# Plain projection pairs by single channel tile in two PSUM banks, and three more pairs by seven products, in an encoder layer

## Chip, cores and metric

The kernel runs on one core of one Trainium2 chip. The metric is the device time of one execution in microseconds (us); lower is better. The time before is a median of three runs.

## Reference: what is computed

One layer of an encoder over 1024 + 256 tokens of width 2048, in float32:

```python
h    = rmsnorm(x, norm_w)
P    = h @ w_in          # q, k, v, gate for the neighbourhood attention (4 x 1024 columns),
                         # qk (2048), v, o, z for the mLSTM (3 x 1024), and 16 gate columns
att  = neighbourhood_attention(q, k, v, bias) * silu(gate)        # 8 heads of 128
mem  = rmsnorm(bidirectional_mlstm(silu(conv(qk)), v, gates)) * sigmoid(o) * silu(z)   # 4 heads of 256
y    = rmsnorm(x + concat(att, mem) @ w_out, final_norm_w)
```

## The kernel before

All matrix products take float32 operands split into a high and a low part, and each product is three matmuls (high by high, high by low, low by high). The 1280 tokens are two groups: group A with 768 tokens and group B with 512. The projection's columns for q, k, gate, qk, o and z are 56 channel tiles of 128 columns, handled two at a time as a pair named by its first tile: QT0 = 0 (attention q), KT0 = 8 (k), GT0 = 16 (gate), QK0 = 24 (mLSTM qk), OT0 = 40, ZT0 = 48. The value columns come in eight units of `proj_v`.

The program has these stages, in this order on TensorE:

1. **Group A, seven products.** `first_tiles` (L282) does pairs 0 and 2 plainly. `pair_a` (L464) does all others with Strassen's seven products of half-size blocks instead of eight; pairs 4 and 6 (QT0 + 4 and QT0 + 6) are its first two. For each of four weight pieces GpSimd forms sums of blocks (L508). For the pairs listed in `SECOND` (L38) the sums 5, 6, 7 and 3 are also stored to DRAM (`sD`, L522), one DMA of 128 KB each, sixteen for a pair. The finished pair is post-processed while the next one runs.
2. **Group B, start.** `proj_v(4)` and `proj_v(0)`, the plain pair 0, and the mLSTM's gates (L1437 to L1443).
3. **Group B, seven products.** `pair_s` (L1338) does the nine pairs of `SECOND`. Each of seven steps loads 512 KB, either a block of the weights or a stored sum, and issues 24 matmuls of 256 columns (L1375), 168 for a pair.
4. **Group B, plain, together with the attention and the mLSTM.** `proj_v` (L705) issues 192 matmuls of 256 columns per unit. `proj_pair` (L646) takes both channel tiles of a pair at once: for each of four weight pieces of 512 KB it splits two halves and issues 24 matmuls of 512 columns (L658), alternating between two PSUM banks, 96 for a pair. The attention (`na_sample`, `na_prompt`) and the mLSTM (`ml_units`) are cut into short units, which `run` (L1300) emits with high priority; the plain pairs and values are emitted earlier with low priority. A scheduler orders each engine's instructions when the program is built: plain matmuls fill TensorE between the steps of the units. Four `late_gate` calls (L691), two plain pairs each, come last and can also be drawn forward as filler.
5. **Output projection.** `product` (L1603) with two rounds of seven products, 1680 matmuls of 512 columns (L1609). Its operands are read back from DRAM by `mix_block` (L1486) on GpSimd's DMA queue into the memory that the attention's tiles held before.

PSUM has eight banks in two pools: tag `pr` with three, tag `a` with five (L73). Stages 1 and 3 and the plain pairs use `pr`; the attention and the mLSTM use `a`, as does every second pair of stage 3. An attention block takes banks for its scores (L767), its transposed probabilities (L783) and its outputs (L820 for the sample, L878 for the prompt). A head's query and key tile (`nqk`, L793 and L838) has one buffer: the loads for the prompt part of a head can start only when the sample part's scores are done, and the other way round.

The square in the mLSTM's output norm (L1254) writes an unused result into a tile of the pool `sml`, which has six buffers and also holds the gate operands that are loaded from DRAM.

Of the kernel before, what the change touches and what calls it, by code (L numbers as in the profile page):

```python
# [38 lines left out]
    GT0, QK0 + 8, GT0 + 2, QK0, KT0, GT0 + 4, KT0 + 2, GT0 + 6, KT0 + 4,  # L39
# [6 lines left out]
def kernel(  # L46
# [26 lines left out]
    def bank(tag, name):  # L73
        return ps.tile([P, 512], F32, tag=tag, name=name, bufs=3 if tag == "pr" else 5)
# [207 lines left out]
    def first_tiles():  # L282
        names = ("pr", "pr", "pr", "a", "a", "a", "a", "a")
# [362 lines left out]
    def proj_pair(n1, X, late=False):  # L646
        pb = [bank("pr", f"pc{n1}_{j}") for j in range(2)]
        for r in range(4):
            raw = w_piece(w_in[n1 // 2, r], f"{n1}_{r}")
            t = [w_split(raw, j * 512, j * 512 + 512, f"{n1}_{r}{j}") for j in range(2)]  # L650
            for f_ in range(2):
                for q in range(2):
                    xs = X.get(8 * f_ + 2 * r + q)
                    c = (2 * f_ + q) * P
                    first, last = r + f_ + q == 0, r == 3 and f_ == 1 and q == 1
                    for j, passes in enumerate((FORTH, FORTH[::-1])):
                        for m, (wi, xi) in enumerate(passes):
                            PE.matmul(  # L658
                                pb[j], t[j][:, wi, c : c + P], xs[xi],
                                start=first and m == 0, stop=last and m == 2,  # L660
                            )
        out = []
        for j in range(2):
            o = po(f"pco{n1}_{j}")
            if QK0 <= n1 < OT0:
                ct = n1 - QK0 + j
                DM.dma_start(o[:, 0:4], qb[ct])
                for z in (260, 518):
                    G.memset(o[:, z : z + 2], 0.0)
                out_scaled(  # L670
                    o[:, 4:].rearrange("p (s c) -> p s c", s=2)[:, :, :256],
                    pb[j].rearrange("p (s c) -> p s c", s=2),
                    rbs[1].rearrange("p (s c) -> p s c", s=2), n1,
                )
                for _ in conv_b(o, ct):
                    pass
                continue
            o = o[:, :GB]
            out_scaled(o, pb[j], rbs[1], n1)
# [25 lines left out]
    def proj_v(u, X):  # L705
# [54 lines left out]
    def sml(name, n=256, dt=F32):  # L760
        return ap.tile([P, 260], dt, tag="sml", name=name, bufs=6)[:, :n]
# [29 lines left out]
    def na_sample(h):  # L791
# [28 lines left out]
        b = bank("a", f"{nm}o")  # L820
# [12 lines left out]
    def na_prompt(h):  # L833
# [13 lines left out]
        def block(c4):  # L847
# [30 lines left out]
            b = bank("a", f"{n2}o")  # L878
# [173 lines left out]
    def ml_units(sq, h, gates):  # L1052
# [98 lines left out]
        def out_unit(J):  # L1151
# [84 lines left out]
            for e in range(2):  # L1236
# [17 lines left out]
                jk = sml(f"{n2}jk{e}")  # L1254
# [83 lines left out]
    def pair_s(n1, tag, bg):  # L1338
        nm = f"S{n1}"
        bx, by, bz = (bank(tag, f"{nm}b{i}") for i in "xyz")  # L1340
# [105 lines left out]
    for i, n in enumerate(SECOND):  # L1446
        bg = pair_s(n, ("pr", "a")[i % 2], bg)
# [4 lines left out]
    for i in range(ML_H):  # L1452
        for u in (("v", 4 + i), QK0 + 8 + 2 * i, QK0 + 2 * i, ("v", i), QT0 + 2 * i, KT0 + 2 * i):
# [3 lines left out]
            elif u not in SECOND and u != QT0:  # L1457
                proj_pair(u, X)
    def paced(units, n):
# [182 lines left out]
    slots = iter(("aaaaa" "ppp") * 8)  # L1642

    def p_banks(p, j):
        return [bank("pr" if next(slots) == "p" else "a", f"po{p}_{j}_{i}") for i in range(NT)]
# [130 lines left out]
```

## Time and profile before

| What | Value |
|---|---|
| Median of three runs | 2568.87 us (2566.79 to 2569.39) |
| The profiled execution | 2567.36 us |
| Span from its first to its last instruction | 2565.5 us |
| Mean granted TensorE clock | 0.998 |
| TensorE matmul busy | 2534.0 us (99%) |
| VectorE busy | 1968.9 us (77%) |
| ScalarE busy | 1336.5 us (52%) |
| GpSimd busy | 610.6 us (24%) |
| DMA traffic | 503.03 MB |

In the profile, PE is TensorE's matmuls, PEld its weight loads, DVE is VectorE, ACT is ScalarE, POOL is GpSimd and SPq the queue of the sync engine, which issues most DMAs. PEclk is the clock that TensorE was granted, 1.00 being full. A line such as L658 is the line of the program above. The view of the chain follows the work that ended last back to its start; the view of the waits adds up the idle time of an engine by what ended it; the view of windows gives each engine's busy time in stretches of the span, with the share of the time in which the 16 DMA engines were busy.

### The profile page before, as it was taken

To read this page: it belongs to the slowest core of one execution; us is meant where nothing else is said; L and a number is where in the kernel's file an instruction comes from. 1 tells how busy PE (TensorE), PEld (TensorE's weight loads), DVE (VectorE), ACT (ScalarE), POOL (GpSimd) and SP (SyncE) were. 2 spreads that over 40 slices of the span, in tenths; PEclk is the share of its full clock that TensorE was granted. 3 is DMA by queue.
4 is the path that set the end of the run, shared out by engine and by line. 5 is a ranking of instruction groups with operands and counts; after the bars stand their busy time and mean duration, and the time that the engine had idled before them with its cause. 6 is when DMAs were issued, how large, how long until landed. Compare 5 with 4: busy or idle time off the path is not lost.

```text
span 2565.5 us, 44500 instructions
## 1 busy us (share of the span) xinstructions
PE 2534.0 (99%) x15054; PEld 2367.4 (92%) x15054; DVE 1968.9 (77%) x4029; ACT 1336.5 (52%) x3041; POOL 610.6 (24%) x909
## 2 busy tenths in 40 slices
PE   8999999999999999999999999999999999999998
PEld 8999999999999999999999999899988887788886
DVE  8768878888978798888875875876855665879695
ACT  8534544444444444475655665665745553344444
POOL 0434555444444444510000000100100104000001
PEclk9999999999999999999999999999999999999999
DMA  6545454635433332476778877978867839636227
GB/s 214 170 145 183 155 182 139 185 114 189 138 120 124 105 130 102 134 245 214 230 235 292 284 250 266 304 234 275 286 199 249 280 126 374 204 128 215 85 87 254
DMA packets 303483, 503.03 MB, mean 196 GB/s; under 512 B 48752, under 2 KB 191256, under 8 KB 303256
## 3 DMA queue, kind: packets, MB, share of 16 engines
q1 hardware_dynamic: 299096, 484.46, 57.4%
q0 software_dynamic: 4160, 15.73, 1.6%
q8 instruction: 119, 1.95, 0.3%
q14 instruction: 108, 0.88, 0.1%
HBM read 373.13 MB, written 126.95 MB: 195 GB/s over the span
## 4 chain that ended last, share of the span: by engine, by line
PE 77%; DMA 3%; DVE 2%; ACT 0%; issue 0%; SPq 0%; POOL 0%; ACTq 0%; POOLq 0%; DVEq 0%
PE pc L658 16%; PE po L1609 15%; PE pv L736 5%; PE A52b L274 1%; PE A44b L274 1%; PE A40b L274 1%; PE A48b L274 1%; PE A20b L274 1%; PE A50b L274 1%; PE A42b L274 1%; PE A18b L274 1%; PE A54b L274 1%; PE A70b L274 1%; PE A68b L274 1%; PE A36b L274 1%; PE A46b L274 1%
## 5 line engine op out<-in xcount | busy, mean ns | idle before, releaser
L1609 PE MATMUL po<-wo,mo 128*128 128x512 f32 x1620 | 377.8, 394 | 2.5 <-ACT wo L165 2.2
L1609 PEld LDWEIGHTS po<-wo,mo 128*128 128x128 f32 x1620 | 305.0, 188 | 74.5 <-ACT wo L165 3.0
L166 DVE TENSOR_TENSOR ws<-wr,ws 128x512 fp32r<-128x512 f32 x152 | 105.0, 700 | 50.8 <-ACT ws L165 50.1
L165 ACT CAST ws<-wr 128x512 fp32r<-128x512 f32 x152 | 92.5, 617 | 68.0 <-PE pc L658 56.0
L165 ACT CAST mo<-mb 128x640 fp32r<-128x640 f32 x72 | 52.0, 726 | 97.4 <-PE po L1609 79.1
L116 POOL TENSOR_SCALAR rs<-rs 128x1 f32<-128x1 f32 x10 | 3.4, 342 | 350.4 <-DVE rs L1589 350.3
L166 DVE TENSOR_TENSOR mo<-mb,mo 128x640 fp32r<-128x640 f32 x72 | 58.6, 820 | 30.5 <-ACT mo L165 30.2
L1558 DVE TENSOR_TENSOR y<-y,po 128x512 f32<-128x512 f32 x90 | 58.3, 682 | 11.7 <-PE po L1609 11.5
L165 ACT CAST mo<-ms 128x640 fp32r<-128x640 f32 x40 | 28.9, 726 | 59.7 <-PE po L1609 34.2
L166 DVE TENSOR_TENSOR wsv<-wr_v,wsv 128x512 fp32r<-128x512 f32 x64 | 44.4, 699 | 12.6 <-ACT wsv L165 12.4
L165 ACT CAST wsv<-wr_v 128x512 fp32r<-128x512 f32 x64 | 38.9, 616 | 22.7 <-PE pv L736 11.5
L413 DVE SCALAR_TENSOR_TENSOR pcv<-pco,cw_sb,pcv 128x516 f32<-128x516 f32 x48 | 36.3, 757 | 8.0 <-ACT pcv L407 7.9
L1572 ACT ACTIVATE jk<-y 128x512 f32<-128x512 f32 x40 | 25.2, 631 | 33.0 <-DVE y L1558 32.8
L166 DVE TENSOR_TENSOR mo<-ms,mo 128x640 fp32r<-128x640 f32 x40 | 32.7, 819 | 8.0 <-ACT mo L165 7.8
L129 ACT ACTIVATE xq<-xq 128x1024 f32<-128x1024 f32 x20 | 21.2, 1061 | 29.6 <-DMA xq<-in_xtok_dram 27.1
L1077 POOL MEMSET mls_0v<- 128x2 f32 x4 | 0.4, 102 | 145.0 <-DVE S_dt.float L166 119.9
L274 PE MATMUL fb<-xg,fw 128*128 128x384 f32 x192 | 34.6, 334 | 0.0
L251 DVE TENSOR_TENSOR pco<-pc,rstdb 128x512 f32<-128x512 f32 x30 | 20.6, 686 | 18.0 <-PE pc L658 17.9
L274 PEld LDWEIGHTS fb<-xg,fw 128*128 128x128 f32 x192 | 33.4, 188 | 0.0
L1521 DVE TENSOR_TENSOR ms<-mb,mb 128x640 f32<-128x640 f32 x40 | 32.7, 818 | 0.0
L774 DVE CUSTOM_DVE_ANT_0 nap_0st<-nap_0s,nap_0bt 128x384 f32<-128x384 f32 x32 | 17.7, 554 | 19.2 <-PE nap_0s L769 8.7
L1488 POOL DMA_DIRECT2D mb<-mx x32 | 17.7, 556 | 59.1 <-DVE ws L166 24.7
(2655 smaller groups left out, 8497.4 us busy)
## 6 DMA issues: line engine op xcount, KB each, us to landing
wr<-in_w_in_dram SPq DMA_DIRECT2D x76, 512.0 KB, 4.4
wr_v<-in_w_in_dram SPq DMA_DIRECT2D x32, 512.0 KB, 4.6
wb<-in_w_o_dram SPq DMA_DIRECT2D x48, 256.0 KB, 3.1
xq<-in_xtok_dram SPq DMA_DIRECT2D x20, 512.0 KB, 4.3
mb<-mx POOLq DMA_DIRECT2D x32, 320.0 KB, 8.2
wr_wp<-in_w_o_dram SPq DMA_DIRECT2D x16, 512.0 KB, 3.8
vS<-vo SPq DMA_DIRECT2D x24, 256.0 KB, 4.9
nap_0bt<-in_rpb_tab_dram SPq DMA_DIRECT2D x32, 192.0 KB, 4.1
```

The lines of the kernel that those rows point to most:

```text
L129: S.activation(raw, raw, AF.Square, accum_out=ssq[g][:, t, q : q + 1])
L165: S.copy(hi, src)
L166: V.tensor_tensor(lo, src, f(hi), op=ALU.subtract)
L251: V.tensor_tensor(o, src, rb, op=ALU.mult)
L274: PE.matmul(o, w(a_), x(b_), start=first and m == 0, stop=last and m == 2)
L413: V.scalar_tensor_tensor(dst[:, a:n], src[:, a + j - pad : n + j - pad], cw_sb[:, ct, j : j + 1], dst[:, a:n], op0=ALU.mult, op1=ALU.add,)
L658: PE.matmul(pb[j], t[j][:, wi, c : c + P], xs[xi], start=first and m == 0, stop=last and m == 2,)
L736: PE.matmul(outs[tt], xs[:, tt * P : (tt + 1) * P], t[:, wi, q * w : (q + 1) * w], start=first and m == 0 and (gates or tt % 2 == 0), stop ...
L1521: V.tensor_tensor(t, x, y_, op=op)
L1558: V.tensor_tensor(Y[p, q, tt], Y[p, q, tt], bk, op=op)
L1572: S.activation(jk, Y[p, q, tt], AF.Square, accum_out=ss[t][:, c : c + 1])
L1609: PE.matmul(bk[tt], m[xi][:, tt * P : (tt + 1) * P], w[wi], start=first and kk == 0 and j == 0, stop=last and j == 2, skip_group_check=True,)
```

## The change

Three more pairs (KT0 + 6, QT0 + 4 and QT0 + 6) join `SECOND`: their sums are stored in stage 1 and they are done by seven products in stage 3. `proj_pair` does one channel tile after the other, each in one bank of `pr`, and loads half a pair's columns for two pieces at a time. `pr` has two banks, and the third becomes a tag of its own, `m`, for the attention's outputs and wherever three banks were taken together. The square gets a tile of its own, `sml` has seven buffers instead of six, and the stores of `proj_v` are emitted with high priority.

```diff
 SECOND = (
-    GT0, QK0 + 8, GT0 + 2, QK0, KT0, GT0 + 4, KT0 + 2, GT0 + 6, KT0 + 4,
+    GT0, QK0 + 8, GT0 + 2, QK0, KT0, GT0 + 4, KT0 + 2, GT0 + 6, KT0 + 4, KT0 + 6, QT0 + 4, QT0 + 6,
 )
...
-        return ps.tile([P, 512], F32, tag=tag, name=name, bufs=3 if tag == "pr" else 5)
+        return ps.tile([P, 512], F32, tag=tag, name=name, bufs={"pr": 2, "m": 1, "a": 5}[tag])
...
-        tags = ("pr", "pr", "pr", "a", "a", "a", "a")
+        tags = ("pr", "pr", "m", "a", "a", "a", "a")
...
     def proj_pair(n1, X, late=False):
-        pb = [bank("pr", f"pc{n1}_{j}") for j in range(2)]
-        for r in range(4):
-            raw = w_piece(w_in[n1 // 2, r], f"{n1}_{r}")
-            t = [w_split(raw, j * 512, j * 512 + 512, f"{n1}_{r}{j}") for j in range(2)]
-            for f_ in range(2):
-                for q in range(2):
-                    xs = X.get(8 * f_ + 2 * r + q)
-                    c = (2 * f_ + q) * P
-                    first, last = r + f_ + q == 0, r == 3 and f_ == 1 and q == 1
-                    for j, passes in enumerate((FORTH, FORTH[::-1])):
-                        for m, (wi, xi) in enumerate(passes):
-                            PE.matmul(
-                                pb[j], t[j][:, wi, c : c + P], xs[xi],
-                                start=first and m == 0, stop=last and m == 2,
-                            )
         out = []
         for j in range(2):
+            pb = bank("m" if n1 + j == QT0 else "pr", f"pc{n1}_{j}")
+            for r in range(4):
+                if r % 2 == 0:
+                    raw = w_piece(
+                        w_in[n1 // 2, r : r + 2, :, j * 512 : (j + 1) * 512].rearrange(
+                            "r p c -> p r c"
+                        ),
+                        f"{n1}_{j}{r}",
+                    )
+                t = w_split(raw, r % 2 * 512, r % 2 * 512 + 512, f"{n1}_{j}{r}")
+                for fq in range(4):
+                    f_, q = divmod(fq, 2)
+                    xs = X.get(8 * f_ + 2 * r + q)
+                    first, last = r + fq == 0, r + fq == 6
+                    for m, (wi, xi) in enumerate(FORTH[:: (1, -1)[fq % 2]]):
+                        PE.matmul(
+                            pb, t[:, wi, fq * P : fq * P + P], xs[xi],
+                            start=first and m == 0, stop=last and m == 2,
+                        )
             o = po(f"pco{n1}_{j}")
...
-            store_v(u, GA + tt * P, o, outs[tt][:, :256], rc[:, tt : tt + 1])
+            with tc.high_priority():
+                store_v(u, GA + tt * P, o, outs[tt][:, :256], rc[:, tt : tt + 1])
...
-        return ap.tile([P, 260], dt, tag="sml", name=name, bufs=6)[:, :n]
+        return ap.tile([P, 260], dt, tag="sml", name=name, bufs=7)[:, :n]
...
-        b = bank("a", f"{nm}o")
+        b = bank("m", f"{nm}o")
...
-            b = bank("a", f"{n2}o")
+            b = bank("m", f"{n2}o")
...
-                jk = sml(f"{n2}jk{e}")
+                jk = ap.tile([P, 256], F32, tag="jk", name=f"{n2}jk{e}", bufs=1)
...
-        bg = pair_s(n, ("pr", "a")[i % 2], bg)
+        bg = pair_s(n, (("pr", "pr", "m"), ("a", "a", "a"))[i % 2], bg)
...
-    slots = iter(("aaaaa" "ppp") * 8)
+    slots = iter((("a",) * 5 + ("pr", "pr", "m")) * 8)
```

`first_tiles` (L283) takes the same banks under the new tags, and `pair_s` gets the three tags instead of one.

More of the change, by code (lines that the diff above doesn't have):

```diff
@@ L678, in proj_pair @@
             o = o[:, :GB]
-            out_scaled(o, pb[j], rbs[1], n1)
+            out_scaled(o, pb, rbs[1], n1)
             if n1 < GT0:
@@ L1640, in product @@
             each(tt)
-    slots = iter(("aaaaa" "ppp") * 8)
+    slots = iter((("a",) * 5 + ("pr", "pr", "m")) * 8)
     def p_banks(p, j):
-        return [bank("pr" if next(slots) == "p" else "a", f"po{p}_{j}_{i}") for i in range(NT)]
+        return [bank(next(slots), f"po{p}_{j}_{i}") for i in range(NT)]
     for i in range(4):
```

8 lines of the change are left out of this document (4 added, 4 removed).

## The prediction

> **What bounds the kernel now.** I read the page first, then the waits of TensorE, then the chain in order of time, then the windows by stage. The page's busy shares and clock:
>
> ```profile
> span 2565.5 us, 44500 instructions
> PE 2534.0 (99%) x15054; PEld 2367.4 (92%) x15054; DVE 1968.9 (77%) x4029; ACT 1336.5 (52%) x3041; POOL 610.6 (24%) x909
> ```
>
> A busy PE alone proves little, since matmul ends are modelled. The waits of TensorE between 1380 and 2170 us (plain work, attention and mLSTM) say more: four kinds, 3.6 us in all.
>
> ```profile
> PE nap_0s L769 <- DMA nap3qk<-kS: 1.9, 1, 1.9
> PE mls_0s L1091 <- DVE mls_0d L1190: 1.0, 1, 1.0
> PE nap_0s L769 <- DMA nap2qk<-kS: 0.5, 1, 0.5
> PE nap_0s L769 <- DMA nap4qk<-kS: 0.2, 1, 0.2
> ```
>
> So TensorE's own work sets the time, and a matmul taken away is time taken away as long as nothing new is waited for. The chain gives the price of the matmuls (start, length, instruction count):
>
> ```profile
> 632.06 29.13 PE A32b L274 x168
> ...
> 1180.31 2.83 PE S16bx L1375 x24
> ...
> 1202.29 2.84 PE S32bx L1375 x24
> ...
> 1221.58 2.84 PE S18bx L1375 x24
> ...
> 1356.71 10.60 PE pv L736 x90
> ...
> 1631.91 9.61 DMA nap3qk<-kS
> ...
> 1894.49 36.60 PE pc L658 x158
> ...
> 2116.14 39.53 PE pc L658 x170
> 2156.36 14.33 DMA wr_wp<-in_w_o_dram
> 2171.44 21.25 PE po L1609 x84
> ```
>
> The reader is to see that the undisturbed run of 158 plain matmuls goes at 36.60/158 = 0.2316 us each, and that from pair 32 (1202.29) to the first value matmul (1356.71) lie eight seven-product pairs in 154.42 us: 19.30 us a pair, 0.1149 us a matmul, with no stall between pairs (32 to 18 is 19.29 too). The windows by stage (start:end, length; busy PE, PEld, DVE, ACT, POOL; PEclk; DMA share; GB/s):
>
> ```profile
> 1202.00:1357.00 155.00, 155.00 (x1351) 155.00 (x1350) 121.63 (x212) 90.47 (x172) 0.26 (x4) 1.00 0.69 225
> 1357.00:2116.00 759.00, 755.24 (x4831) 684.48 (x4829) 513.43 (x1396) 448.77 (x1114) 67.73 (x252) 1.00 0.77 256
> 2116.00:2162.00 46.00, 46.00 (x200) 37.32 (x199) 25.47 (x38) 15.20 (x25) 19.95 (x36) 1.00 0.94 364
> 2162.00:2171.00 9.00, 7.59 (x33) 5.82 (x31) 5.45 (x8) 2.32 (x4) 4.39 (x8) 1.00 1.04 390
> 2171.00:2180.00 9.00, 8.56 (x30) 6.89 (x31) 3.54 (x6) 2.67 (x5) 3.30 (x6) 0.81 1.03 386
> ```
>
> Nothing else is full: DVE 68% and ACT 59% in the attention stage, DMA 77%. The nearest rival is DMA.
>
> **The change part by part.** *Three pairs by seven products.* A plain pair is 96 matmuls by 0.2316 = 22.24 us; by seven products it is 19.30. Three pairs save 3 × 2.94 = **8.8 us**. All of it lies on TensorE's path. The rows of eight such pairs show no wait, with both bank sets in turn, so I give the three new ones (4 is on the `pr`, `pr`, `m` banks, 14 and 6 on `a`) the same price. Bound: pair 16, which has the mLSTM gates' work among its matmuls, took 1202.29 − 1180.31 = 21.98 us; at that price the three would save only 0.8 us.
>
> The Trainium skill ("TensorE: Matmul & The Clock Gate", section on the back-to-back issue gap) gives a fixed start-to-start cost of about 2.5 ns on top of N/2.4 ns, which speaks against 72 more and shorter matmuls a pair. By it a pair would go from 20.7 to 18.3 us, an estimate from that page, and three would save 7.1 us. The rows show no such cost: 2 × 0.1149 = 0.2298 is no more than 0.2316, so the rows decide.
>
> *Stored sums in stage 1.* The sums are formed by GpSimd already; new are 48 stores, 32 of them in the first two pairs of stage 1. The DMA issues (KB each, median us to landing) and the two waits of these pairs:
>
> ```profile
> sD<-A24t SPq DMA_DIRECT2D x16, 128.0 KB, 3.1
> ```
>
> ```profile
> PE A4b L274 <- DVE A4s L173: 1.6, 1, 1.6
> PE A6b L274 <- ACT A4c L479: 1.1, 1, 1.1
> ```
>
> In the changed order the stores stand on SP's queue between the loads for pairs 4 and 6, so a load now also waits for GpSimd's sums ahead of it, and a sum's buffer is held 3.1 us longer. From the order, every weight load is still passed at least 5 us of matmuls before its first use. I put 0.5 us, between −1.1 (pair 6 now runs products 6 and 5 in the other order, which could remove that wait) and +2.7 (both waits double). The reading back is in the 19.30 us.
>
> *Less cover in the attention.* This is the real question. In the program's order, the stretch from the first matmul of `proj_v(5)` to the last attention matmul holds 1528 plain matmuls before and 1076 after: 288 went to stage 3, 164 more now stand behind the attention (200 plain matmuls there before, 364 after). The stretch shrinks by 452 × 0.2316 = 104.7 us, from 759.4 to 654.7 us. One reason is visible: at 1894.49 TensorE does 158 plain matmuls without any attention, since heads 6 and 7 wait for their q and k, which now come in stage 3. The rest is that outputs have their own bank. So DVE and ACT rise to at most 513/655 = 78% and 449/655 = 69%, still not bounds, as their filler work moves out too. The DMAs were busy 0.77 × 759 = 584 us; 4.7 fewer pairs take away 4.7 × 2 MB, at 256/0.77 = 332 GB/s some 28 us, which leaves 556 of 655, 85%. The stretch from 2116 to 2162 shows TensorE fully busy at 0.94, so 85% alone stops nothing; what counts is how late single loads come.
>
> The latest is the key load of a head's prompt part: its buffer comes free when the sample scores are read. The work between those scores and the first prompt scores, counted in program order at the measured cadences (384 columns 29.13/168 = 0.173 us), was 10.8, 11.7 and 10.9 us for heads 2, 3 and 4, which then still waited 0.5, 1.9 and 0.2; the data came 11.3, 13.6 and 11.1 us after the release. Five heads with 10.9 to 20.4 us never waited. After, the eight distances are 10.0, 11.8, 9.7, 12.3, 10.2, 12.0, 14.2 and 12.5 us. If each load takes 11.2 us, the waits are 1.2 + 1.5 + 1.0 = 3.7 us, 1.1 more than now. If each takes 13.6, they are 3.6 + 1.8 + 3.9 + 1.3 + 3.4 + 1.6 + 0 + 1.1 = 16.7 us, **14.1 more**. If none is late, 2.6 fewer. I take 1.1, nearest to most heads.
>
> *Thin places and the one output bank.* The timeline around 1704 us:
>
> ```profile
> 1704.03 0.33 PE L897 MATMUL nap_1o<-nap_1pt,nap_1v 128*128 128x128 f32 x2
> ...
> 1704.40 0.48 ACT L788 CAST nap_2pt<-nap_0t 128x384 fp32r<-128x384 f32 x1 [0.26 <-PE nap_1o L897]
> ...
> 1704.78 0.41 DVE L902 TENSOR_TENSOR nap_1os<-nap_1os,nap_1o 128x256 f32<-128x256 f32 x1
> ...
> 1705.44 0.55 DVE L789 TENSOR_TENSOR nap_2pt<-nap_0t,nap_2pt 128x384 fp32r<-128x384 f32 x1
> ```
>
> The output bank is free 0.83 us after its last matmul (1704.36 to 1705.19); in the changed order the next output starts at least 4.2 us later, so one bank costs nothing; DVE would have to run 3 us behind. Scores to transposes keep at least 5.7 us (7.7 before). Two places are thin: a sample's transposes to its output 0.46 us, and an mLSTM transpose to its state product 0.58 us, where copy and subtraction take 1.6 us (1704.40 to 1705.99). I add 2 × 1.1 = 2.2 us, between −1.0 (the 1.0 wait goes too) and +2.2.
>
> *Plain pairs by tile.* Same matmuls, same four loads of 512 KB, in rows of 2 KB instead of 4 KB; the bank of the tile before last is reused after at least 3.1 us of other work, against an eviction of 0.69 (mean of 30, below). Nothing. *Own tile for the square, seven buffers, stores first*: these only let ACT and SP go earlier; nothing, and what they hide stays hidden by TensorE's queue.
>
> ```profile
> L251 DVE TENSOR_TENSOR pco<-pc,rstdb 128x512 f32<-128x512 f32 x30 | 20.6, 686 | 18.0 <-PE pc L658 17.9
> ```
>
> *Start of the output projection.* The operands' loads begin when the attention's memory is free:
>
> ```profile
> 2120.50 4.01 POOL L1488 DMA_DIRECT2D mb<-mx  x7 [24.75 <-DVE ws L166]
> ...
> 2176.75 0.56 POOL L1566 DMA_DIRECT2D y<-in_xtok_dram  x1 [0.56 <-PE po L1609]
> ```
>
> ```profile
> PE po L1609 <- ACT wo L165: 2.2, 2, 1.8
> PE po L1609 <- DVE wo L166: 0.4, 1, 0.4
> ```
>
> That is 56 us of issuing, with the DMAs full, while only 46 us of plain work stand behind the attention; then TensorE waits 2.6 us in three places, 1.8 of it at 2170, and from 2171 to 2180 the clock is 0.81, another 0.19 × 9 = 1.7 us: 4.3 us in all. After, 364 × 0.2316 = 84 us of plain work cover it. I take half, **2.1 us** gained, between 0 and 4.3.
>
> The sum: −8.8 + 0.5 + 1.1 + 2.2 − 2.1 = −7.1. The profiled execution took 2567.36 us (span 2565.5 and 1.9 around it), so 2560.3; it lies 1.5 below the median 2568.87 of runs that spread over 2.6, so I predict **2561**.
>
> **Rivals.** *Late key loads (slower).* The denser stage makes every prompt's key load as late as head 3's: +14.1 us of waits in place of 1.1. For it: the load's 9.6 us at 1631.91 and a DMA share rising to 85%. Three waits exceed 3.4 us, and if each brings the clock dip of 2171 (1.7 us), 5.1 more: 2560.3 + 13.0 + 5.1 = 2578. It beats the saving once a load takes over some 12.8 us. Against it: five of eight heads are faster today, and the wait of 1.9 us, in this window, brought no dip (clock 1.00):
>
> ```profile
> 1600.00:1650.00 50.00, 48.08 (x307) 43.44 (x306) 40.71 (x100) 31.38 (x79) 6.46 (x20) 1.00 0.92 307
> ```
>
> The Trainium skill ("TensorE: Matmul & The Clock Gate", Part 1, the HAM clock gate) has the array fall to half clock after an idle window of about 3.4 us. The dip to 0.81 after 1.8 us of idling agrees in kind; the size is from the row.
>
> *The gain is eaten (no change).* The new pairs cost what pair 16 cost, or the key loads take 13 us: 2560.3 + 8.0 = 2568, or 2564 to 2572 in parts. For it: 3.5 MB of loads a pair beside the post-processing; against it, eight pairs in a row at 19.30.
>
> *More than forecast.* No wait in the attention (−3.6 instead of +3.3) and the whole 4.3 us at the output projection: 2560.3 − 6.9 − 2.2 = 2551. The shares of DMA speak against the first.
>
> **How the numbers follow.** Forecast (2556 to 2564) 0.60, more 0.10, eaten 0.19, late loads 0.11. Faster by over 0.2%, 5.1 us, about what a measurement of this kernel can tell, is the first two: 0.70; within it 0.19; slower 0.11. The range leaves out the far part of the late loads and most of the gains beyond: 2555 to 2570.
>
> **What would show it.** Twelve pairs at 19.3 us, the attention stage about 655 us long with TensorE waits of 4 to 8 us, mainly for key loads; the output projection starting without the idle 1.8 us and without the 0.81. Wrong would be: waits over 12 us in the attention, new pairs over 20 us, waits in pairs 4 and 6 over 5 us, or DMA waits of the plain pieces in rows of 2 KB.

## The result, and the profile after

The changed kernel took 2586.14 us (median of four runs, 2584.38 to 2588.62) against 2569.13 us for the kernel before (four runs, 2566.79 to 2569.69): a ratio of 1.0064, 95% interval 1.0051 to 1.0077. It is 17 us slower; 8 us faster was forecast. The profiled execution took 2588.62 us, the longest of the four, 21.3 us more than that of before.

```profile
span 2586.9 us, 45144 instructions
...
PE 2537.6 (98%) x15270; PEld 2380.7 (92%) x15270; DVE 1978.0 (76%) x4062; ACT 1344.5 (52%) x3071; POOL 609.9 (24%) x909
```

TensorE's busy time rose by 3.6 us although 8.8 us of matmuls went: some of it ran at a lower clock. The chain of waits in stage 3 shows that the saving itself is there (start, length):

```profile
1367.20 2.84 PE S14bx L1380 x24
...
1386.50 2.84 PE S4bx L1380 x24
...
1405.79 2.84 PE S6bx L1380 x24
```

The new pairs follow each other at 19.30 and 19.29 us, as forecast. To find the loss I split the span at four instants that both kernels have, from the tiles' first and last matmuls: pair 16 in stage 1, the first value matmul of group B, the last matmul by seven products, and the first matmul of the output projection.

| | before | after | difference |
|---|---|---|---|
| start of pair 16, stage 1 | 452.9 | 464.5 | +11.6 |
| first value matmul (B) | 1103.8 | 1115.2 | +11.4 |
| last seven-product matmul | 1356.4 | 1424.8 | +10.5 beyond three pairs of 19.30 |
| from there to the output projection | 806.1 | 760.0 | 66.7 less work, 46.1 less time: 20.6 lost |
| output projection to the end | 403.0 | 402.1 | -0.9 |

So +10.5 + 20.6 - 0.9 - 8.8 = +21.4, the difference of the spans (2586.9 - 2565.5). I call the fourth stretch the attention stage, and "lost" its time beyond 806.1 us less 22.23 us for each plain pair that left it.

**The opening of stage 1.** The window from 60 to 165 us, before and after (columns as in the prediction), and the waits of TensorE from 60 to 125 us after:

```profile
60.00:165.00 105.00, 102.04 (x575) 99.09 (x575) 75.63 (x153) 52.42 (x125) 45.21 (x52) 1.00 0.58 183
```

```profile
60.00:165.00 105.00, 97.16 (x523) 93.89 (x521) 70.44 (x142) 50.09 (x118) 42.92 (x47) 0.95 0.66 206
```

```profile
PE A6b L274 <- ACT A4c L479: 2.9, 1, 2.9
PE A4b L274 <- DVE fo L381: 2.1, 1, 2.1
PE A4b L274 <- DVE A4s L173: 1.7, 1, 1.7
```

4.9 us more idle time, and a lower clock, 0.95 over the 105 us, which cost another 4.5 us of working time. The second part was in no term of my sum. It follows the waits; us by us after the wait of 2.1 us that ended at 78.2:

```profile
80.00:81.00 1.00, 1.00 (x5) 1.00 (x4) 0.83 (x3) 0.97 (x3) 0.71 (x1) 0.50 0.65 229
...
82.00:83.00 1.00, 1.00 (x5) 1.00 (x5) 0.00 (x0) 0.00 (x0) 1.00 (x3) 0.50 0.99 274
83.00:84.00 1.00, 1.00 (x6) 1.00 (x5) 0.00 (x0) 0.29 (x1) 0.44 (x1) 0.83 0.75 281
```

TensorE looks fully busy here: a busy share doesn't show that each matmul takes twice as long. The dip costs about 1.7 us on top of the wait. Where the delay begins can be read from SP's queue, after and then before:

```profile
65.48 2.02 SPq L522 DMA_DIRECT2D sD<-A4t  x3
67.60 1.38 SPq L128 DMA_DIRECT2D xq<-in_xtok_dram  x2
...
75.60 0.33 SPq L503 DMA_DIRECT2D A4r<-in_w_in_dram  x1
```

```profile
65.21 5.52 SPq L128 DMA_DIRECT2D xq<-in_xtok_dram  x3
73.17 0.33 SPq L503 DMA_DIRECT2D A4r<-in_w_in_dram  x1
```

After, two loads of tokens (`xq`) stand behind stores of sums and are issued at 67.60 in place of 65.21 us. ScalarE, which squares the tokens, began on the first of them at 72.34 in place of 69.23, and its casts and VectorE's copies behind it came later too. The wait of 2.1 us is for such a copy (`fo`), which frees a PSUM bank; the longest one, 2.9 us, is for ScalarE's copy `A4c`, which frees another. The waits for the split weights themselves (`A4s`, `A6s`) grew by only 1.1 us.

**The attention stage.** The whole stage before and after, then the longest waits of after in it:

```profile
1356.40:2162.50 806.10, 802.34 (x5036) 722.77 (x5035) 539.50 (x1435) 464.36 (x1141) 87.75 (x289) 1.00 0.78 262
```

```profile
1424.80:2184.80 760.00, 744.08 (x4748) 675.84 (x4747) 509.98 (x1395) 439.55 (x1104) 90.24 (x293) 0.99 0.81 266
```

```profile
PE nap_0s L774 <- DMA nap0qk<-kS: 6.1, 1, 6.1
PE mls_0s L1096 <- DMA mls_0q<-cS: 2.7, 2, 2.4
PE mls_0s L1096 <- DMA mlp_2or<-pT: 2.0, 1, 2.0
PE mls_0s L1096 <- issue: 1.2, 1, 1.2
PE mlp_1in L1096 <- ACT mlp_1x L1225: 1.0, 1, 1.0
PE mlp_1in L1096 <- DVE nap_0pt L794: 0.7, 1, 0.7
```

Idle time is 760.00 - 744.08 = 15.9 us where it was 3.8, so 12.1 of the 20.6 us are waits. Four clock dips make most of the other 8.5. They stand behind the gaps of 6.1, 2.0 and 2.4 us and one of 1.2 and 0.6 close together:

```profile
1452.00:1458.00 6.00, 2.20 (x7) 2.13 (x8) 1.18 (x4) 0.02 (x1) 0.91 (x2) 0.51 1.04 396
1592.00:1600.00 8.00, 6.25 (x31) 5.42 (x30) 7.63 (x25) 5.20 (x16) 1.30 (x2) 0.79 0.48 135
1760.00:1767.00 7.00, 5.05 (x31) 4.87 (x30) 3.16 (x10) 0.99 (x4) 0.62 (x2) 0.76 1.00 324
1930.00:1940.00 10.00, 7.59 (x51) 7.39 (x51) 3.96 (x14) 4.58 (x16) 0.00 (x0) 0.83 0.91 298
```

Length by missing clock is 1.6 + 1.7 + 1.7 + 1.7 = 6.7 us, counting in the first row only the work after the gap (1455.8 to 1459.0 us, clock 0.51), since the gap itself is in the 15.9 already. The last 1.8 us aren't explained. The key loads of heads 1 to 7, where I had placed 2.5 us of waits, cost 0.2; head 0's alone cost 6.1. The timeline from its sample's last scores to the prompt's first, after:

```profile
1438.72 0.52 PE L774 MATMUL nas_1s<-nas0qk 128*128 128x256 f32 x3
...
1455.80 1.30 PE L774 MATMUL nap_0s<-nap0qk 128*128 128x384 f32 x3 [6.10 <-DMA nap0qk<-kS]
```

```profile
1445.20 0.95 SPq L845 DMA_DIRECT2D nap0qk<-qS  x1
1446.20 0.60 SPq L846 DMA_DIRECT2D nap0qk<-kS  x1
```

and the same tiles before (range of starts in each row):

```profile
L769 PE MATMUL nas_1s<-nas0qk x3: 282/283/285, 1369.9 to 1370.1; 128*128 128x256 f32 x3
...
L841 SPq DMA_DIRECT2D nap0qk<-kS x1: 607/607/607, 1377.5 to 1377.5; - x1
DMA to landing us min/median/max: 7.8/7.8/7.8
...
L769 PE MATMUL nap_0s<-nap0qk x12: 331/336/338, 1391.0 to 1430.0; 128*128 128x384 f32 x12
```

In both kernels the load of the keys is issued 7 us after the scores and lands 7.8 us later before, 9.5 after: 14.9 and 16.5 us from release to landing. Before, 20.4 us of work stood between, so it was late for nobody; after, 10.5 us (10.0 in the prediction's count).

### The profile page after: what moved, and what is told of

Read it like the earlier page. It is cut to its first block, busy times and chain, and to the rows that moved or that the text cites. A ratio compares the mean times of both kernels' runs of the same rounds, so it can differ in the third digit from the quotient of the medians.

```text
span 2586.9 us, 45144 instructions
## 1 busy us (share of the span) xinstructions
PE 2537.6 (98%) x15270; PEld 2380.7 (92%) x15270; DVE 1978.0 (76%) x4062; ACT 1344.5 (52%) x3071; POOL 609.9 (24%) x909
## 4 chain that ended last, share of the span: by engine, by line
PE 71%; DMA 6%; DVE 3%; issue 1%; SPq 1%; ACT 0%; ACTq 0%; POOL 0%; POOLq 0%; DVEq 0%
PE pc L664 13%; PE po L1615 11%; PE pv L740 5%; PE A52b L274 1%; PE A48b L274 1%; PE A44b L274 1%; PE A40b L274 1%; PE A20b L274 1%; PE A54b L274 1%; PE A50b L274 1%; PE A46b L274 1%; PE A42b L274 1%; PE A18b L274 1%; PE A70b L274 1%; PE A36b L274 1%; PE A66b L274 1%
## 5 line engine op out<-in xcount | busy, mean ns | idle before, releaser
L166 DVE TENSOR_TENSOR ws<-wr,ws 128x512 fp32r<-128x512 f32 x128 | 88.2, 692 | 59.1 <-ACT ws L165 58.7
L165 ACT CAST ws<-wr 128x512 fp32r<-128x512 f32 x128 | 78.5, 617 | 84.9 <-PE pc L664 51.0
L274 PE MATMUL fb<-xb,fw 128*128 128x384 f32 x96 | 23.8, 356 | 7.0 <-ACT fw L172 7.0
L274 PE MATMUL A4b<-xg,A4s 128*128 128x384 f32 x144 | 28.5, 354 | 1.7 <-DVE A4s L173 1.7
```

The costliest lines, as they stand in the source:

```text
L165: S.copy(hi, src)
L166: V.tensor_tensor(lo, src, f(hi), op=ALU.subtract)
L274: PE.matmul(o, w(a_), x(b_), start=first and m == 0, stop=last and m == 2)
```

## The experiments

All ratios are to the kernel before on the same chip. "B" is the first value matmul of group B, "lost" is in the attention stage as above, and "rest" the output projection to the end, all from the one profiled execution. The times of kernels with ten runs spread over some 8 us, and the same stage-1 program began pair 16 at 452.2, 453.6 and 457.0 us in three kernels; so a difference of 5 us between two profiles is not read as an effect.

| run | median us | ratio (95%) | B | lost | rest |
|---|---|---|---|---|---|
| kernel before | 2566 to 2569 | 1 | 1103.8 | 0 | 403.0 |
| changed kernel | 2586.1 | 1.0064 (1.0051-1.0077) | 1115.2 | 20.6 | 402.1 |
| e1 nine pairs | 2570.4 | 1.0014 (1.0005-1.0023) | 1103.0 | 3.7 | 399.8 |
| e2 twelve alone | 2597.1 | 1.0117 (1.0104-1.0131) | 1112.4 | 19.5, 11.7 of it behind the attention | 411.7 |
| e3 calm opening | 2582.6 | 1.0062 (1.0049-1.0075) | 1104.5 | 26.5 | 400.4 |
| e4 sums on GpSimd's queue | 2588.6 | 1.0085 (1.0072-1.0099) | 1112.5 | 23.0 | 401.5 |
| e5 e3 and own q, k | 2578.4 | 1.0049 (1.0034-1.0064) | 1103.8 | 21.1 | 400.6 |
| e6 one bias table | 2581.9 | 1.0055 (1.0040-1.0070) | 1114.3 | 17.4 | 400.6 |
| e7 loads ahead | 2595.2 | 1.0106 (1.0089-1.0123) | 1118.9 | 26.5 | 401.3 |
| e8 sums on ScalarE's queue | 2590.8 | 1.0088 (1.0066-1.0110) | 1112.3 | 20.4 | 400.1 |
| e9 stores on GpSimd's queue | 2576.9 | 1.0036 (1.0027-1.0046) | 1113.2 | 12.9 | 401.5 |
| e10 thin stores | 2583.6 | 1.0055 (1.0040-1.0070) | 1111.9 | 20.8 | 400.4 |
| e11 e3 and e9 | 2574.4 | 1.0021 (1.0011-1.0030) | 1106.9 | 11.3 | 401.0 |
| v_conv3 three convolution pairs | 2569.8 | 1.0010 (1.0000-1.0019) | 1107.6 | 11.8 | 401.4 |
| v_conv3 and own q, k | 2575.1 | 1.0034 (1.0024-1.0044) | 1103.1 | 20.6 | 400.6 |
| v_conv3 and e9 | 2569.3 | 1.0002 (0.9992-1.0011) | 1103.5 | 8.1 | 401.6 |
| the same, values on SP | 2569.6 | 1.0004 (0.9995-1.0013) | 1104.4 | 13.7 | 401.2 |
| before, stores on GpSimd | 2577.9 | 1.0036 (1.0024-1.0048) | 1105.7 | 6.3 | 404.7 |
| before, ten pairs | 2579.6 | 1.0041 (1.0027-1.0055) | 1102.3 | 9.1 | 411.3 |

### List or other edits: e1 and e2

e1 is the changed kernel with the old list, e2 the kernel before with the new list:

```diff
-    GT0, ..., KT0 + 4, KT0 + 6, QT0 + 4, QT0 + 6,
+    GT0, ..., KT0 + 4,
```

> The changed kernel with only nine pairs by seven products, all other edits kept. In the changed kernel's profile stage 1 ended 11.4 us later than before (first value matmul of group B at 1115.2 against 1103.85) and the attention stretch lost 20.7 us against its own work in waits and clock. Theory: the first loss comes from the stores of pairs 4 and 6 in the opening, the second from the density of the attention stretch. Then stage 1 here is as before (first value matmul within 1.5 us of 1103.9), the stretch, with 1406 plain matmuls in it instead of 1076 (1528 before), loses between 4 and 12 us, and the time is 0 to 10 us above before. Rival: the banks, the pairs by single tile and the small edits make the loss; then the stretch loses 15 us or more here too and the time is 15 to 25 us above before.

> The kernel before with only the list of seven-product pairs lengthened to twelve. Theory: the opening loses the same 10 to 12 us, stage 3 gains 8.8, the attention stretch has 1371 plain matmuls in it (1076 in the changed kernel, 1528 before) and loses 4 to 12 us: 5 to 15 us above before, 5 to 12 below the changed kernel. Rival (banks and single tiles make the stretch's loss): the stretch loses no more than before (3.6 us) and the time is within 4 us of before.

e1 came out 4.4 us above the kernel before: without the longer list the other edits cost little. e2 was 31 us above it, far beyond the 5 to 15 expected. The list alone brings the opening's loss (B at 1112.4). What I had not seen is its end: only 69 plain matmuls stand behind its attention, and the output projection then waits for its operands. Its first wait, and below it the waits in the same place with ten pairs:

```profile
PE po L1609 <- issue: 11.7, 1, 11.7
```

```profile
PE po L1609 <- ACT wo L165: 5.1, 2, 3.8
```

The view names no releaser for the 11.7 us ("issue"), but ScalarE's cast of the weights just before had waited 11.4 us for their load. The wait ends with the first matmul of the output projection, so it stands in the 19.5 us: in the attention itself e2 lost 7.8 us, within the 4 to 12 expected, nearly all of it the key wait of head 0 (6.0 us) and the dip behind it. So the list alone brings head 0's wait, which e1 doesn't have. But neither the list alone (7.8) nor the other edits alone (3.7) lose what both together lose there (20.6).

With 299 or more plain matmuls behind the attention "rest" is 400 to 402 us, with 200 it is 403.0 (405 in a second kernel), with 188 and 69 it is 411 to 412. So the edits other than the list bring what they are good for, a longer tail; which of them does is not shown, and the 12 matmuls between 200 and 188, 2.8 us of work, don't by themselves explain a step of 8 us.

### The opening: e3, e4, e7, e8, e10

e3 swaps the pairs that open stage 1:

```diff
-    order = [4, 6]
-    rest = list(range(KT0, QK0, 2)) + list(range(OT0, NCH, 2))
+    order = [OT0, OT0 + 2]
+    rest = list(range(KT0, QK0, 2)) + [4, 6] + list(range(OT0 + 4, NCH, 2))
```

> The changed kernel with another order in stage 1: two pairs of o tiles, which store no sums, open it instead of pairs 4 and 6, which come later. Theory (the stores hurt only in the crowded opening, where SP's queue holds them between the first loads): the first value matmul of group B comes 8 to 11 us earlier than in the changed kernel, at 1104 to 1107, and the time is 7 to 12 us below it. Rival (the stores cost wherever they are, by their traffic): it comes within 3 us of 1115 and the time stays within 4 us of the changed kernel.

The opening came back whole (B at 1104.5), with the same stores later in stage 1. So it is their place at the opening that costs, not the stores as such. But little of it reached the end, where the theory had the time 7 to 12 us lower: the attention stage lost 26.5 us, and the ratio is the same as the changed kernel's within the intervals.

e4 and e8 take the stores off SP's queue (`DM.dma_start` at L522 becomes `G.` or `S.dma_start`):

> The changed kernel with the stores of the sums issued on GpSimd's queue, where the sums are formed, instead of SP's. Theory (a store that waits for its sum holds up the loads behind it on SP's queue): the opening gets back 5 to 11 us. Rival (it is the traffic, or the sums' buffers held until the store has landed): it gets back less than 3 us.

> The changed kernel with the 48 new and 144 old stores of sums in stage 1 issued on ScalarE's queue in place of SP's, ahead of the cast that needs the same sum anyway; bytes and buffers as in the changed kernel. The run with the stores on GpSimd's queue put 0.56 us of issuing on GpSimd for each store, ahead of the next sum, and so didn't settle the cause. Theory, that loads of weights and of x stand on SP's queue behind stores that wait for sums: pair 16 starts by 457 us (464.5 in the changed kernel, 452.9 before), TensorE waits under 4 us in pairs 4 and 6 in place of 7.7, and the total is 5 to 9 below the changed kernel. Rival, that the stores' traffic or the sums' buffers held until they land cost the time: pair 16 starts after 461, and the waits stay at 6 or more.

Pair 16 began at 458.6 and 460.3 us (464.5 in the changed kernel, 452.9 before): 4 to 6 of the 11.6 us came back, about as much as the spread named above, and under 3 us of it were left at B. For e4 the theory asked for 5 to 11 and the rival for under 3; e8's start lies between the bounds of its two theories, and its waits in pairs 4 and 6, 6.8 us, are what its rival said. Neither kernel was faster than the changed one. Each queue has a price of its own. On GpSimd each issue stands between two sums:

```profile
66.65 0.73 POOL L508 TENSOR_TENSOR A4t<-A4r 128x256 f32<-128x256 f32 x1
67.33 0.56 POOL L522 DMA_DIRECT2D sD<-A4t  x1
67.91 0.79 POOL L508 TENSOR_TENSOR A4t<-A4r,A4t 128x256 f32<-128x256 f32 x1
```

On ScalarE a cast stands behind a store that waits for a sum of the next pair. e7 was to load each piece one piece ahead:

```diff
+            if n1 == 4 or n1 == 6 and r < 3:
+                a_raw(*((n1, r + 1) if r < 3 else (6, 0)), keep=True)
```

> The changed kernel with each weight piece of pairs 4 and 6 loaded one piece ahead, in front of the stores of the piece before on SP's queue; the 32 stores stay. Theory, that a load stands on SP's queue behind stores that wait for GpSimd's sums, which wait for the load before: pair 16 starts at 453 to 457 us in place of 464.5, as early as in the kernel before (452.9), and the first value matmul of the attention's stretch lies at 1104 to 1107 instead of 1115. Rival, that the traffic of the stores itself, or the sums' buffers held until they land, delays the pairs: pair 16 still starts after 461. The time of the whole follows the opening at most: 2574 to 2579 by the theory if the attention stage stays as in the changed kernel, 2583 or more by the rival; the run with the calm opening lost 4 to 6 us of what it had won in the attention stage, so up to 2584 speaks against neither.

It did the opposite: the order that was built issued the second piece at 82.50 us (75.60 in the changed kernel) and pair 16 began at 467.7. It tells nothing of the cause. e10 leaves the places and takes the bytes:

```diff
-                    DM.dma_start(sD[n1, i][:, r * 256 : (r + 1) * 256], src[i])
+                    w_ = 8 if n1 in (4, 6) else 256
+                    DM.dma_start(sD[n1, i][:, r * 256 : r * 256 + w_], src[i][:, :w_])
...
-                DM.dma_start(raw, sD[n1, i])
+                DM.dma_start(raw, sD[14 if n1 in (4, 6) else n1, i])
```

> The changed kernel, in which the 32 stores of sums of pairs 4 and 6 carry 8 of 256 columns, at the same places of the same queue; later these two pairs read the sums of pair 14, so the output isn't the reference's. Issues, waits of the queue and buffers' order stay, 4 MB of traffic go. Theory, that the stores' places cost (a load on SP's queue behind a store that waits for a sum, a sum's buffer held until its store has landed): pair 16 starts at 460 us or later, as in the changed kernel (464.5), and TensorE waits 6 us or more in pairs 4 and 6. Rival, that the traffic of the stores delays the loads: pair 16 starts by 457 and the waits fall under 4.

Pair 16 began at 460.3, and these waits were left:

```profile
PE A4b L274 <- DVE fo L381: 2.5, 1, 2.5
PE A6b L274 <- ACT A4c L479: 2.4, 1, 2.4
```

Without the bytes, 7.4 of the 11.6 us stay, and the 4.1 that came back are within the spread: the theory of the places holds for the larger part. SP's queue stands still for the stores' sums as long as in the changed kernel (15.3 and 14.8 us there between 60 and 135 us; the queue's own waits in e10):

```profile
SPq L523 <- POOL A4t L508: 16.6, 13, 6.0
SPq L523 <- POOL A6t L508: 14.7, 11, 3.0
```

How the 7 us divide between SP's queue and the four buffers of the sums stays open; a ring of eight wasn't tried.

### The attention: key buffer and traffic, e5 and e6

e5 gives the sample's q and k a tile of their own, on top of e3:

```diff
-        qk = na_tile("nqk", [P, 4, TP], f"{nm}qk", 1, F32R)[:, :, :TS]
+        qk = na_tile("nqs", [P, 4, TS], f"{nm}qk", 1, F32R)
```

> The changed kernel with pairs 48 and 50 at the opening (as in the run before, which took 2582.6 against 2566.0 for the kernel before), and with the sample's q and k in a tile of their own, so that the key load of the prompt part no longer waits until the sample scores are read; one of eight buffers of the mLSTM state ring pays for the space. Theory, that the buffer makes the key loads late: the wait of 5.3 us at head 0 goes with its clock dip of about 2, the other key waits go too, and the time is 7 to 9 below that run, 2574 to 2576. Rival, that all the loads of the denser attention stage are late together: something else is late in its place (mLSTM operands, value or bias loads), less than 4 is gained, 2579 to 2584.

Head 0's wait of 5.3 us went, and no other key load of a prompt part was waited for. But the median fell only by 4.2 us, 21.1 us were still lost, and these came in its place:

```profile
PE mlp0a3tb L1121 <- DMA mlp0a3cv<-cD: 3.2, 1, 3.2
PE mlp2a2kv L1096 <- DVE mlp2a2w L169: 2.5, 1, 2.5
```

Between the two theories, nearer to the rival. But `mlp2a2w` is a tile of the ring that e5 makes one buffer shorter, and no run separates that price from the gain of the key tile. In e6 one bias table serves all blocks:

```diff
+        if "t" not in one:
+            one["t"] = na_tile("nbt", [P, NAK], f"{nm}bt", 1)
+            DM.dma_start(one["t"], rpb_tab[0, :, :NAK])
```

> The changed kernel with one bias table that is loaded once and used for every block and head, in place of one load per block: it leaves out the other bias tables, so its output isn't the reference's. Some 15 MB of loads go out of the attention stage; the tile's order of work stays. Theory, that the DMAs' load in the denser stage (shares of 0.93 to 0.99) makes its loads late: TensorE's waits there fall from 15.6 to under 6 us, the stage loses under 9 us over its own work in place of 20.7, and the time is about 12 below the changed kernel, 1.000 to 1.003 of the kernel before. Rival, that each late load is late for its own buffer or its own place in the queue: the same loads are waited for, 12 us or more, and the ratio stays at 1.005 or above.

The theory that the stage's traffic makes the loads late fell. The whole attention stage, then its two longest waits:

```profile
1425.00:2181.80 756.80, 741.07 (x4748) 672.33 (x4747) 508.96 (x1395) 441.82 (x1104) 88.73 (x294) 1.00 0.76 248
```

```profile
PE nap_0s L776 <- DMA nap0qk<-kS: 4.7, 1, 4.7
PE mls_0s L1100 <- DMA mls_0q<-cS: 3.4, 3, 1.8
```

The DMAs' share is 0.76, less than in the kernel before (0.78), and 17.4 us are still lost, with the same two waits at the top. But this is a mean: around head 0's key load the DMAs are full in e6 too (share 1.02 from 1430 to 1456 us; 1.05 in the changed kernel, and 1.06 from 1362 to 1386 us in the kernel before, where nobody waited). So e6 takes away the traffic of the stage, not that of this place.

### Which pairs: v_conv3, and its own q and k

```diff
-    GT0, ..., KT0 + 4, KT0 + 6, QT0 + 4, QT0 + 6,
+    GT0, ..., KT0 + 4, QK0 + 10, QK0 + 2, QK0 + 12,
```

> The changed kernel, but the three pairs that join the list of seven products are mLSTM convolution pairs (34, 26 and 36) instead of attention keys and queries (14, 4 and 6), so the opening of stage 1 is that of the kernel before, and heads 6 and 7 keep their plain work in the attention; 1115 plain matmuls stand in the stretch and 325 behind it. Theory, that the loss comes from the stores in the opening pairs and from attention work that has lost its plain matmuls between key loads: the opening costs under 2 us, the key loads have distances of 10.7 to 13.1 us, the attention stage loses under 8, and the time is 2560 to 2567, that is 0.998 to 1.001 of the kernel before. Rival, that any three pairs fewer in the stretch make its loads late: the stage loses 15 us or more over its own work, and the time is 2572 or more, a ratio of 1.003 or above.

Three convolution pairs save the same 8.8 us, with no store at the opening. The ratio, 1.0010, is the upper edge of the theory's range, but the median of 2569.8 us is above it, and 11.8 us are lost, between the theory's 8 and the rival's 15. With the tile of e5 on top:

> The run with the three convolution pairs (2569.8 against 2567.5 for the kernel before, a ratio of 1.001; 11.7 us lost from the end of the seven-product pairs to the output projection), with the sample's q and k in a tile of their own and one buffer fewer in the mLSTM state ring. Theory, that what is left of the loss are loads that wait for a buffer: the loss falls to 8 or less and the time is 2562 to 2566, a ratio of 0.998 to 0.9995. Rival, that the work closes up in time by what the buffer gives (1082 plain matmuls in the stretch in place of 1115) and waits elsewhere: a ratio of 1.000 to 1.002.

Both ranges were missed: 5 us slower, and 20.6 us lost. Freed from the key tile's buffer (and again with the shorter ring), the order that is built closes up: 1082 plain matmuls stand among the attention in place of 1115 and 358 behind it in place of 325. Of its longest waits the first stood in the run without the tile too (2.9 us), the second, for VectorE, and the third, for a load, are new:

```profile
PE mls_0s L1096 <- DMA nas0qk<-qS: 3.2, 1, 3.2
PE mlp3a2kv L1096 <- DVE mlp3a2w L169: 2.7, 1, 2.7
PE mlp0a3tb L1121 <- DMA mlp0a3cv<-cD: 2.1, 1, 2.1
```

### Loads behind stores, or less work between loads: e9, e11 and three more

e9 issues the stores of the later stages on GpSimd's queue:

```diff
+    ST[0] = G
     operand_sums()
...
-            DM.dma_start(vS[u][t0 : t0 + P], flat)
+            ST[0].dma_start(vS[u][t0 : t0 + P], flat)
```

> The changed kernel with the stores of the later stages' tiles (queries, keys, values, convolution, gates; from the second operand sums on) on GpSimd's queue in place of SP's; the loads stay on SP. From the end of the seven-product pairs to the first matmul of the output projection the kernel before took 806.1 us, 66.7 of it the plain work that went; the changed kernel took 760.0 in place of 739.4, a loss of 20.6. Theory, that loads on SP's queue wait behind stores whose data isn't ready: the loss falls to 10 or less, the key wait of head 0 goes, and the time is 10 or more below the changed kernel. Rival, that each load is late by its own buffer's release and its landing time, and that the queue isn't the bound (its issues fill under half of the stage): the loss stays at 15 to 22.

> The changed kernel with both: pairs 48 and 50 at the opening of stage 1 instead of 4 and 6, and the later stages' stores on GpSimd's queue. Theory, that the two losses are separate and add: the first value matmul lies at 1103 to 1106, the loss after the seven-product pairs is 11 to 15, and the time is 2566 to 2570, a ratio of 0.9995 to 1.0015. Rival, that whatever comes earlier is waited away again in the attention, as in the run with the calm opening alone (a loss of 26.5 there): a loss of 18 or more and a ratio of 1.003 or above.

> The run with the three convolution pairs (2569.8, a ratio of 1.001; 11.7 us lost after the seven-product pairs), with the later stages' stores on GpSimd's queue, which took 8 of 20.6 us of that loss away in the changed kernel. Theory, that loads behind waiting stores on SP's queue are the common cause: the loss falls to 6 or less and the time is 2559 to 2565, a ratio of 0.997 to 0.9995, below both kernels. Rival, that what the queue gave there came from the other distribution of the plain work (head 0's distance rose from 10.0 to 21.1 us): here the loss stays at 9 or more and the ratio at 1.000 to 1.002.

e9 won 8 of the 20.6 us, short of its theory. e11 agrees with separate losses on what is lost (11.3), and lies a little outside on B and on the time: of the 16 us above the kernel before, 11 are gone. The combination with convolution pairs reached 1.0002, the ratio of its rival, with 8.1 us lost in its fastest execution, 5 us below its median. But e9 doesn't show that stores block loads. At head 0 of e9:

```profile
L775 PE MATMUL nas_1s<-nas0qk x3: 278/282/282, 1437.7 to 1437.9; 128*128 128x256 f32 x3
```

```profile
L847 SPq DMA_DIRECT2D nap0qk<-kS x1: 603/603/603, 1446.0 to 1446.0; - x1
```

The key load was issued 7.8 us after the sample's scores (1437.9 + 0.3), no earlier than in the two kernels above; its wait went because the order that was built has 21.1 us of work there in place of 10.0. A wait of 3.8 us for a tile of values (`vo`) stands there instead. Two runs asked this directly:

> The last run with three convolution pairs and the later stages' stores on GpSimd's queue (a ratio of 1.0002, 7.9 us lost after the seven-product pairs), with the stores of the values back on SP's queue: 4.1 us of its waits were for values' tiles (plain and value matmuls behind their evictions) that stay in use until GpSimd's queue has sent them. Theory, that these waits are the price of the other queue: the loss falls to 5 or less and the ratio to 0.9975 to 0.9993, below both kernels. Rival, that SP's loads then wait behind the values' stores again: the loss stays at 7 to 12 and the ratio at 1.000 or above.

> The kernel before with nothing but the same stores of the later stages on GpSimd's queue (the list of nine, the pairs by piece and the banks as they were). It had 3.6 us of waits in that stage. Theory, that SP's waiting stores cost where plain work is thin between loads, which it hardly is here: a ratio of 0.9985 to 1.0005. Rival, that the queue is a gain by itself, whatever the change: 0.998 or below.

The values' stores back on SP's queue changed nothing that can be measured (1.0004 against 1.0002; the losses of the two profiles, 13.7 and 8.1, differ about as their executions do, 2570.7 and 2564.1 us). And in the kernel before the other queue costs 9 us, which neither theory foresaw. It is no gain by itself: it helps where it happens to put work in front of a late load.

> The kernel before with a single convolution pair (38) more in its list and nothing else: 2.9 us of TensorE's work go, 1444 plain matmuls stand in the attention's stretch in place of 1528 and 188 behind it in place of 200. Theory, that the attention stage loses with each plain matmul that leaves it, and not by the other edits: at the mean of the runs so far (3.7 us for 122, 11.7 for 413, 20.6 for 452, that is 0.03 to 0.045 us each) 84 of them cost 2.5 to 4, so the ratio is 0.999 to 1.001. Rival, that small steps are free and only the last ones cost: the whole 2.9 us come out, a ratio of 0.9985 or below.

One convolution pair more in the kernel before makes it 10 us slower: 9.1 us lost in the attention and 8 in "rest", against 2.9 saved. So there is no constant price for a matmul taken out, and small steps aren't free either. The loss does rise with the plain matmuls that are gone from the attention's stretch, though: 3.7 us with 1406 left (e1), 7.8 with 1371 (e2), 8 to 14 with 1141 to 1112 (five kernels), 17 to 27 with 1082 to 1056 (nine kernels). Ten pairs (9.1 with 1444) and the kernel before with the other queue (6.3 with 1528) stand outside this order. No run of the study beat the kernel before; the best two lie within 0.1% of it.

## Why the prediction was wrong

- *Three pairs by seven products*: -8.8 forecast, -8.8 measured. Right, and the doubt from pair 16's 21.98 us didn't come true.
- *Stored sums in stage 1*: **+0.5 forecast, +10.5 to 11.6 measured**, outside the bounds (-1.1 to +2.7). The step failed at "every weight load is still passed at least 5 us of matmuls before its first use": this counts work in program order, takes it that SP gets to the load in time, and looks at weight loads alone. In fact the stores ahead of the loads wait for GpSimd's sums; the tokens' loads were issued at 67.60 in place of 65.21 us, the second weight piece of pair 4 at 75.60 in place of 73.17, the last two at 89.93 in place of 85.40. TensorE's longest new waits are for copies that free banks, the first of them held up by the late tokens. The wait of 1.1 us that the other order of products was to remove grew to 2.9. I doubled two waits as the upper bound (5.4 us; they came to 7.7) and left out the clock's answer, 4.5 us.
- *Less cover in the attention*: **+1.1 forecast, and together with "Thin places" 3.3, 20.6 measured**. I had named the right place, but failed in two steps. First, the time from release to landing was taken from heads 2 to 4 (11 to 13.6 us), because only their waits were visible. Head 0 needed 14.9 us already in the kernel before, hidden under its 20.4, and it was head 0 that lost 10 us of cover. Second, I asked only for the key loads; waits for other loads in the mLSTM came to 4.7 us more, and e5 shows that when one load is helped another is late. The clock's answer to these waits, 6.7 us, was in the rival and not in this term.
- *Late key loads (slower)*, the rival with 0.11, came nearest to the time (2578), with the clock dips it spoke of. Its mechanism was half right: one key load, not each, and half of the waits elsewhere. Its other sign, the rising DMA share (0.81 measured, 85% forecast), isn't the reason by e6, as far as the mean of the stage goes.
- *Thin places and the one output bank*: 2.2 forecast. The two places that I named (a sample's transposes to its output, an mLSTM transpose to its state product) aren't among the waits at all; others, for the mLSTM's `mlp_1in` and an output of the attention, come to 2.3 us. The size is right by luck.
- *Plain pairs by tile, own tile, seven buffers, stores first*: 0 forecast. e1 has all of them and loses 3.7 us in the attention and wins 3.2 in "rest": 0 within what these profiles can tell.
- *Start of the output projection*: -2.1 forecast, -0.9 measured, inside the bounds. The first stall and its dip went, others of 2.4 us came later.

The Trainium skill ("TensorE: Matmul & The Clock Gate", Part 1) lets the array fall to half clock after an idle window of about 3.4 us, and back after a busy one as long. The trace agrees in the clock (0.50) and in how long a dip lasts (80.0 to some 83.3 us). But shorter gaps were enough here, 2.0 to 2.9 us in the changed kernel and 1.8 us at 2171 in the kernel before, while one of 2.5 us at 367 in the changed kernel brought no dip. So the 1.9 us that I had quoted as harmless was no safe bound.

What is shown: the list brings the opening's loss (e1, e2), which goes when its stores don't stand there (e3), and most of it isn't bytes (e10). That SP's queue is the reason is read from the trace; e4 and e8, which take the stores off it, don't show it. In the attention the list alone brings head 0's wait, and the rest of the loss takes the list and the other edits together (e1, e2). It isn't the stage's traffic (e6), and helping one load or one queue moves it elsewhere (e5, v_conv3 with its own q and k, before with the stores on GpSimd). That the common cause is too little work between a load's release and its use fits the order by plain matmuls above, but no run shows it by itself, since none could set those distances alone. Why e3 lost 26.5 us and one pair alone 9.1 stays open.

## What to carry to other kernels

When TensorE is the bound, its own filler may also be what hides the loads, as these runs suggest: price a matmul taken away together with every load it covered, and take a load's lateness from release to landing on each instance, above all on those where it is hidden today. Look for stores that wait for data and are put ahead of loads on the same queue: here the loads behind them were issued 2.4 to 4.5 us later. And add to each new wait of some 2 us or more the clock that it may cost afterwards.

## What the runs showed of the hardware

The granted clock fell to 0.50 in dips of some 3.4 or 6.8 us, which cost up to half of that. In all 19 profiles, from 30 us on, every wait of TensorE over 2.6 us met such a dip; of the waits between 1.6 and 2.6 us some did and some didn't. In the changed kernel the dips cost about 4.5 us in the opening, where 4.9 us of waits were added, and 6.7 in the attention, with 12.1. And the time to landing of a store hardly depends on its size here; the issues of the sums in the changed kernel and in e10:

```profile
sD<-A4t SPq DMA_DIRECT2D x16, 128.0 KB, 2.6
```

```profile
sD<-A4t SPq DMA_DIRECT2D x16, 4.0 KB, 2.6
```
